# Fifteen small loads at the head of ScalarE's DMA queue in a streaming row-normalisation kernel

## The chip, the cores and the metric

The kernel runs on one core of one Trainium2 chip. The metric is device time in microseconds (us). The times shown are whole-launch times; the span of a profile runs from the first to the last instruction of one profiled execution.

## The reference

The input `x` has the shape (32, 512, 1024) in float32, that is 16384 rows of 1024 elements, 67.11 MB. Each row is divided by the sum of its absolute values, and the result has the same shape.

```
sums = np.sum(np.abs(x), axis=-1, keepdims=True)
return (x / (sums + 1e-8)).astype(np.float32)
```

## The kernel before

All of `x` is read once and all of the output is written once. The 16384 rows are 128 for each of 128 partitions. They are cut into eleven pieces: ten with 12 rows per partition (6144 KB) and a last one with 8 rows per partition (4096 KB). Pieces 0, 1 and 10 lie in the first 32 x 128 rows of the input, where partition p owns 32 rows one after the other; each of the others is a block of 12 x 128 rows. In this text piece i's load is called L0 to L10 and its store S0 to S10.

One loop runs over the pieces. A piece gets one of four buffers (`BUFS = 4`, tile `x_tile`, 48 KB per partition). SyncE issues the load (line 88). VectorE (DVE) then takes the row sums of absolute values (line 52), adds the epsilon (line 59), takes the reciprocal (line 61) and multiplies most rows in place (lines 63 and 70); ScalarE (ACT) multiplies a few rows of the first three and the last two pieces (line 73, by the table `split`). ScalarE then issues the store (line 91). So loads stand in SyncE's DMA queue, called q1 in the profile, and stores in ScalarE's, called q10. A buffer's next load waits until the store of its last piece has landed, so L4 waits for S0, L5 for S1, and so on.

The order on each engine is the program's order. One more thing sets who waits for whom. Tile, the layer in which the kernel is written, has eight completion semaphores for the DMAs of both queues and gives them out in turn, in the order in which it plans the DMAs; a DMA that takes over a semaphore waits on its engine's queue until the DMA that last had it is complete. In the built program before, the first DMAs have these semaphores, and none of L0 to L3 waits for anything:

```
sem 0: L0   sem 1: L1   sem 2: L2   sem 3: S0
sem 4: L3   sem 5: S1   sem 6: L4   sem 7: S2   then L5 on 0, L6 on 1, ...
```

Of the kernel before, what the change touches and what calls it, by code (L numbers as in the profile page):

```python
# [1 line left out]

# [4 lines left out]

FP32 = mybir.dt.float32
EPS = 1e-8


@with_exitstack
def kernel(
    ctx: ExitStack,
    tc: tile.TileContext,
    x: bass.AP,
    out: bass.AP,
):
    nc = tc.nc
    P = nc.NUM_PARTITIONS  # L20

    x_flat = x.flatten_outer_dims()
    out_flat = out.flatten_outer_dims()
    n, d = x_flat.shape

    R = 12
    BUFS = 4  # L30
    HEAD = 32
    per_partition = n // P
    assert n % P == 0 and (per_partition - HEAD) % R == 0
    rows = [R] * ((per_partition - HEAD) // R + 2) + [HEAD - 2 * R]

    def piece(flat, i):
        head = flat[: P * HEAD, :].rearrange("(p r) d -> p r d", p=P)
        if i < 2:
            return head[:, R * i : R * (i + 1), :]
        if i == len(rows) - 1:  # L40
            return head[:, 2 * R :, :]
        a = P * (HEAD + R * (i - 2))
        return flat[a : a + P * R, :].rearrange("(p r) d -> p r d", p=P)

    sbuf = ctx.enter_context(tc.tile_pool(name="sbuf", bufs=BUFS))
    stats = ctx.enter_context(tc.tile_pool(name="stats", bufs=len(rows)))

    def normalize(x_tile, k, kv, kt):


        s = stats.tile([P, R], FP32)
        nc.vector.tensor_reduce(  # L52
            out=s[:, :k],
            in_=x_tile[:, :k, :],
            axis=mybir.AxisListType.X,
            op=mybir.AluOpType.add,
            apply_absolute_value=True,
        )
        nc.vector.tensor_scalar_add(out=s[:, :k], in0=s[:, :k], scalar1=EPS)  # L59
        inv = stats.tile([P, R], FP32)  # L60
        nc.vector.reciprocal(out=inv[:, :k], in_=s[:, :k])  # L61
        if kv:
            nc.vector.tensor_mul(  # L63
                out=x_tile[:, :kv, :],
                in0=x_tile[:, :kv, :],
                in1=inv[:, :kv].unsqueeze(2).to_broadcast([P, kv, d]),
            )
        for r in range(kv, kv + kt):
            row = x_tile[:, r, :]
            nc.vector.tensor_scalar_mul(out=row, in0=row, scalar1=inv[:, r : r + 1])  # L70
        for r in range(kv + kt, k):
            row = x_tile[:, r, :]
            nc.scalar.activation(  # L73
                out=row,
                in_=row,
                func=mybir.ActivationFunctionType.Copy,
                scale=inv[:, r : r + 1],
            )

    last = len(rows) - 1
    split = {0: (3, 4), 1: (0, 3), 2: (0, 3), last - 1: (0, 2), last: (5, 3)}

    with tc.manual_schedule():
        for i, k in enumerate(rows):
            x_tile = sbuf.tile([P, R, d], FP32)
            nc.sync.dma_start(out=x_tile[:, :k, :], in_=piece(x_flat, i))  # L88
            kt, ks = split.get(i, (0, 0))
            normalize(x_tile, k, k - kt - ks, kt)  # L90
            nc.scalar.dma_start(out=piece(out_flat, i), in_=x_tile[:, :k, :])


# [1 line left out]
_INS = ['x']  # L95
_OUTS = [((32, 512, 1024), 'float32')]


# [23 lines left out]
```

## Time and profile before

| what | value |
|---|---|
| time of the runs | 316.94 and 317.59 us, median 317.26 us |
| span of the profiled execution | 315.8 us |
| VectorE busy | 261.2 us, 83% of the span |
| ScalarE busy | 17.4 us |
| bytes moved | 134.22 MB, 425 GB/s over the span |
| q1 (loads), q10 (stores), share of 16 DMA engines | 49.8% and 49.1% |

The profile's page states no launch time of its own for the profiled execution: what stands beside its span is the median of the runs, 1.46 us above it. The trace holds, beside instructions, a record of every DMA packet: queue, start, duration, bytes. A load or a store of 12 rows is 128 packets of 49152 bytes, one per partition, and sixteen packets of 4 bytes, which raise its completion semaphore.

### The profile page before, as it was taken

The numbers are of one execution on the slowest core, as the hardware profiler recorded it, in microseconds if no ns is written. First come the engines' busy times: TensorE is split into PE (matmuls) and PEld (weight loads), VectorE is DVE, ScalarE is ACT, GpSimd is POOL, SyncE is SP. The second block draws the span as 40 slices with busy tenths as digits, with TensorE's granted clock in tenths as the row PEclk, the third lists the DMA queues.
The fourth block names the chain that finished last, engine by engine and source line by source line (L and its number), as shares of the span: only waits on it lengthen the run. The fifth ranks groups of instructions, "written<-read, shape, count | busy, mean of one in ns | idle before, by whom it ended". The sixth has DMA issues, their size and how long they took to land.

```text
span 315.8 us, 168 instructions
## 1 busy us (share of the span) xinstructions
DVE 261.2 (83%) x51; ACT 17.4 (6%) x16; POOL 0.2 (0%) x4
## 2 busy tenths in 40 slices
DVE  0079999999999999969996999799699969999200
ACT  0010404004000000000000000000000000201200
POOL 0000000000000000000000000000000000000000
DMA  8999999999999999999999999999999999999986
GB/s 324 473 398 448 448 361 430 405 486 405 405 486 405 405 486 411 423 467 405 448 436 411 479 405 411 473 417 405 473 417 411 467 413 450 421 442 423 473 374 282
DMA packets 3168, 134.22 MB, mean 425 GB/s; under 512 B 352, under 2 KB 352, under 8 KB 352
## 3 DMA queue, kind: packets, MB, share of 16 engines
q1 hardware_dynamic: 1584, 67.11, 49.8%
q10 hardware_dynamic: 1584, 67.11, 49.1%
HBM read 67.11 MB, written 67.11 MB: 425 GB/s over the span
## 4 chain that ended last, share of the span: by engine, by line
DVE 41%; DMA 33%; another core or an unknown queue 18%; issue 0%; SPq 0%; DVEq 0%
DVE s L52 23%; DMA x_tile<-in_x_dram 17%; DMA out_dram<-x_tile 16%; DVE x_tile L63 15%; DVE x_tile L70 1%; DVE inv L61 0%; DVE s L59 0%; SPq L88 0%; DVEq L117 0%
## 5 line engine op out<-in xcount | busy, mean ns | idle before, releaser
L52 DVE TENSOR_REDUCE s<-x_tile 128x12 f32<-128x12288 f32 (+1 forms) x11 | 138.2, 12561 | 31.5 <-DMA x_tile<-in_x_dram 31.5
L63 DVE TENSOR_TENSOR x_tile<-x_tile,inv 128x12288 f32<-128x12288 f32 (+3 forms) x10 | 113.6, 11358 | 0.5
L73 ACT ACTIVATE x_tile<-x_tile,inv 128x1024 f32<-128x1024 f32 x15 | 16.1, 1138 | 258.7 <-DVE inv L61 258.7
L70 DVE TENSOR_SCALAR x_tile<-x_tile,inv 128x1024 f32<-128x1024 f32 x8 | 5.5, 748 | 0.0
L61 DVE RECIPROCAL inv<-s 128x12 f32<-128x12 f32 (+1 forms) x11 | 2.5, 226 | 0.4
L73 ACT ACT_TABLE_LOAD x1 | 1.3, 1283 | 17.7 <-DMA x_tile<-in_x_dram 17.7
L59 DVE TENSOR_SCALAR s<-s 128x12 f32<-128x12 f32 (+1 forms) x11 | 1.9, 173 | 0.4
L106 POOL MEMSET const-bfloat16-1.0<- 128x1 bf16 x1 | 0.1, 102 | 0.0
L106 POOL MEMSET const-uint8-127<- 128x1 uint8 x1 | 0.1, 102 | 0.0
L106 POOL MEMSET const-float32-0.0<- 128x1 f32 x1 | 0.1, 99 | 0.2 <-issue 0.2
L106 POOL MEMSET const-float32-1.0<- 128x1 f32 x1 | 0.1, 99 | 0.0
## 6 DMA issues: line engine op xcount, KB each, us to landing
x_tile<-in_x_dram SPq DMA_DIRECT2D x10, 6144.0 KB, 38.0
out_dram<-x_tile ACTq DMA_DIRECT2D x10, 6144.0 KB, 47.4
x_tile<-in_x_dram SPq DMA_DIRECT2D x1, 4096.0 KB, 33.3
out_dram<-x_tile ACTq DMA_DIRECT2D x1, 4096.0 KB, 20.6
```

The costliest lines, as they stand in the source:

```text
L52: nc.vector.tensor_reduce(out=s[:, :k], in_=x_tile[:, :k, :], axis=mybir.AxisListType.X, op=mybir.AluOpType.add, apply_absolute_value=True,)
L59: nc.vector.tensor_scalar_add(out=s[:, :k], in0=s[:, :k], scalar1=EPS)
L61: nc.vector.reciprocal(out=inv[:, :k], in_=s[:, :k])
L63: nc.vector.tensor_mul(out=x_tile[:, :kv, :], in0=x_tile[:, :kv, :], in1=inv[:, :kv].unsqueeze(2).to_broadcast([P, kv, d]),)
L70: nc.vector.tensor_scalar_mul(out=row, in0=row, scalar1=inv[:, r : r + 1])
L73: nc.scalar.activation(out=row, in_=row, func=mybir.ActivationFunctionType.Copy, scale=inv[:, r : r + 1],)
L106: nc = _bacc.Bacc("TRN2", target_bir_lowering=False, num_devices=1)
```

## The change

Before anything else, ScalarE issues fifteen small loads into a new scratch tile `tag`. Number n (called Tn here) copies the first 128 elements of the first n rows of `x`, 512 bytes each, to the first n partitions of `tag`; together they are 120 rows and 61,440 bytes. Nothing reads `tag`.

The loop is also written differently: four loads are written ahead of it, and in it L(i+4) follows S(i). The instructions on SyncE and on VectorE, and their order, are the same as before; ScalarE has the fifteen DMA issues more, ahead of its activation-table load.

```
     with tc.manual_schedule():
-        for i, k in enumerate(rows):
-            x_tile = sbuf.tile([P, R, d], FP32)
-            nc.sync.dma_start(out=x_tile[:, :k, :], in_=piece(x_flat, i))
-            kt, ks = split.get(i, (0, 0))
-            normalize(x_tile, k, k - kt - ks, kt)
-            nc.scalar.dma_start(out=piece(out_flat, i), in_=x_tile[:, :k, :])
+        tag = ctx.enter_context(tc.tile_pool(name="tag", bufs=1)).tile([P, 15, 128], FP32, name="tag")
+        for n in range(1, 16):
+            nc.scalar.dma_start(out=tag[:n, n - 1, :], in_=x_flat[:n, :128])
+        for i in range(BUFS):
+            load(i)
+        for i in range(len(rows)):
+            compute(i)
+            store(i)
+            if i + BUFS < len(rows):
+                load(i + BUFS)
```

`load`, `compute` and `store` hold the same calls as the old loop's body. In the built program after, the fifteen loads take their turns at the eight semaphores too, and waits on SyncE's and ScalarE's queues follow from it:

```
sem 0: T1, T8, L1      sem 1: L0, T9, L2      sem 2: T2, T10, S0     sem 3: T3, T11, L3
sem 4: T4, T12, S1     sem 5: T5, T13, L4     sem 6: T6, T14, S2     sem 7: T7, T15, L5
ScalarE's queue: T1 ... T7 wait for nothing; T8 waits for T1, T9 for L0, T10 for T2, ... T15 for T7
SyncE's queue:   L0 waits for nothing; L1 waits for T8, L2 for T9, L3 for T11
```

From there on each DMA takes over a semaphore from a load or a store well ahead of it, as before.

More of the change, by code (lines that the diff above doesn't have):

```diff
@@ L83, with load, store, compute @@
     split = {0: (3, 4), 1: (0, 3), 2: (0, 3), last - 1: (0, 2), last: (5, 3)}
-    with tc.manual_schedule():
-        for i, k in enumerate(rows):
-            x_tile = sbuf.tile([P, R, d], FP32)
-            nc.sync.dma_start(out=x_tile[:, :k, :], in_=piece(x_flat, i))
-            kt, ks = split.get(i, (0, 0))
-            normalize(x_tile, k, k - kt - ks, kt)
-            nc.scalar.dma_start(out=piece(out_flat, i), in_=x_tile[:, :k, :])
+    tiles = {}
+    def load(i):
+        x_tile = tiles[i] = sbuf.tile([P, R, d], FP32, name="x_tile")
+        nc.sync.dma_start(out=x_tile[:, : rows[i], :], in_=piece(x_flat, i))
+    def store(i):
+        nc.scalar.dma_start(out=piece(out_flat, i), in_=tiles[i][:, : rows[i], :])
+    def compute(i):
+        k = rows[i]
+        kt, ks = split.get(i, (0, 0))
+        normalize(tiles[i], k, k - kt - ks, kt)
+    with tc.manual_schedule():
+        tag = ctx.enter_context(tc.tile_pool(name="tag", bufs=1)).tile([P, 15, 128], FP32, name="tag")
[8 more added lines that the diff above has]
+                load(i + BUFS)
 _INS = ['x']
```

## Prediction

> **What bounds the kernel now.** I began with the page's sliced view, which gives the busy share of each engine in 40 equal slices, and the queue view under it.
>
> ```profile
> span 315.8 us, 168 instructions
> DVE 261.2 (83%) x51; ACT 17.4 (6%) x16; POOL 0.2 (0%) x4
> ...
> DVE  0079999999999999969996999799699969999200
> ...
> DMA  8999999999999999999999999999999999999986
> ...
> q1 hardware_dynamic: 1584, 67.11, 49.8%
> q10 hardware_dynamic: 1584, 67.11, 49.1%
> ```
>
> The reader should see that the DMA row reads 9 from the second slice to the 38th, and that the two queues add to 98.9% of sixteen engines. VectorE has holes, the DMA engines have none. Who waits for whom agrees:
>
> ```profile
> DVE s L52 <- DMA x_tile<-in_x_dram: 31.5, 7, 17.6
> ```
>
> VectorE waits 31.5 us for loads, 17.6 of them for L0; nothing waits long for VectorE. The windowed view, with the DMA share in the next-to-last column and GB/s in the last, shows the same by stage:
>
> ```profile
> 2.00:17.00 15.00, 0.00 (x0) 0.00 (x0) 0.00 (x0) 1.00 0.90 390
> 17.00:20.00 3.00, 2.35 (x1) 1.28 (x1) 0.00 (x0) 1.00 1.02 442
> 20.00:38.00 18.00, 17.90 (x7) 4.27 (x4) 0.00 (x0) 1.00 1.01 437
> ...
> 60.00:120.00 60.00, 59.22 (x10) 3.23 (x3) 0.00 (x0) 1.00 1.01 436
> 120.00:180.00 60.00, 54.22 (x9) 0.00 (x0) 0.00 (x0) 1.00 1.00 433
> ```
>
> (A packet is counted where it starts, hence values beside 1.) The packet records give the bound exactly. A packet of 49152 bytes takes 1.815 us whether it loads or stores, one of 32768 bytes 1.213, one of 4 bytes 0.009. Each engine has 160 of the first, 16 of the second: 160 x 1.815 + 16 x 1.213 = 309.8 us. The first packet starts 1.73 us into the span, the last ends at 314.39, and 1.41 us follow. What is left, 315.8 - 309.8 - 1.7 - 1.4 = 2.9 us, is slow packets: the first of each engine (2.04 to 2.67 us, mean 2.49, so 0.67 over the usual) and the one in which the store queue starts, at 40.5 us (2.94 to 3.61, some 1.2 over), on all sixteen engines, and a few scattered ones of about 2.1 us. So nothing but idle or slower DMA engines can lengthen this kernel, and a stall of all sixteen at any point is added to its end.
>
> **The change part by part.** The sum is made against the profiled execution's span, 315.8 us; the median of the runs, 317.26, is 1.46 higher, and I add the difference to that.
>
> *The loop's new form* moves no instruction on SyncE or VectorE: 0 us.
>
> *The fifteen issues on ScalarE.* A store's issue there takes 0.34 to 0.38 us:
>
> ```profile
> L91 ACTq DMA_DIRECT2D out_dram<-x_tile x11: 338/338/378, 38.7 to 294.1; - x11
> ```
>
> Fifteen are 15 x 0.36 = 5.4 us. ScalarE's first work is a table load at 17.7 us and its first activation at 31.1, when VectorE has the reciprocals:
>
> ```profile
> 17.70 1.28 ACT L73 ACT_TABLE_LOAD   x1 [17.70 <-DMA x_tile<-in_x_dram]
> ...
> 31.10 4.27 ACT L73 ACTIVATE x_tile<-x_tile,inv 128x1024 f32<-128x1024 f32 x4 [12.12 <-DVE inv L61]
> ```
>
> T1 to T7 go out from 0.7 to 3.2 us. T8 follows when T1 has landed. T9 waits for L0 and holds T10 to T15, the table load and the activations behind it: out at 17.6, done issuing at 17.6 + 7 x 0.36 = 20.1, table loaded at 21.4, still 9.7 us ahead of the activation. Cost 0; without VectorE's 13.4 us of sums as cover, 3.7 us.
>
> *Bytes.* No packet of 512 bytes is in the trace. From below it is the 4-byte packet, 0.009 us. From above, it might stall an engine as a queue's first packet does, 0.67 us over. A line through 4 bytes and 49152 bytes gives 0.028 us; I take that, since packets of both sizes follow each other without a gap. With its semaphore packet a tag is 0.037 us per engine. If the engine with most of them gets one row of each, that is 15 x 0.037 = 0.6 us (bounds 0.3 and 10.2). Engines ended between 313.0 and 314.4, so part of this falls into another engine's lead: 0.3 us.
>
> *The wait of L1 for T8*, the dear part. Before, SyncE had all four first loads out at once:
>
> ```profile
> 0.73 1.89 SPq L88 DMA_DIRECT2D x_tile<-in_x_dram  x4
> 17.65 12.95 DVE L52 TENSOR_REDUCE s<-x_tile 128x12 f32<-128x12288 f32 x1 [17.65 <-DMA x_tile<-in_x_dram]
> ```
>
> L1's first packets began the moment L0's last ended, at 16.85 to 17.28 us, mean 17.05. Now L1 is issued only when T8 has landed, and L2 and L3 are queued behind it on SyncE. How long does T8 take? Where both queues hold work, an engine's packet records alternate strictly: one load packet, one store packet, and a 4-byte packet takes a turn of its own. So while L0 is under way, an engine does one packet of a tag for every 1.815 us packet of L0. L0 has eight packets and a semaphore packet on each engine. T1 to T8 have, on an engine that gets a row of each, 8 x 2 = 16 packets. When L0 is done there at about 17, only some 8 of the 16 are. The other 8, tiny, follow at once, 0.2 us, and the semaphore shows 0.35 us later (L0's last 4-byte packets ended up to 17.27, it landed at 17.62). T8 lands at about 17.6, when L0 does.
>
> SyncE then issues L1. From issue to first packet the start of the kernel took 1.0 to 1.64 us, mean 1.14: first packets at 17.62 + 1.14 = 18.76, 1.71 later than before. The rings have run dry, so I charge the first packet's 0.67 again: 1.71 + 0.67 = 2.4 us, bounds 1.7 (soonest start, 0.2 over) and 3.3 (latest, 0.86 over), and nothing if T8 lands before 16.
>
> What is late next? L2 waits for T9, which goes out with L0's landing at 17.6 and meets empty rings: L2 is out by 20 to 24 us, while L1 runs to about 34. L3 needs T11, six more turns of 1.815 at worst, about 30 us, while L2 runs to 48. S0 needs T10, which is there before 38.7. VectorE needs L1 at 38.6 and gets it at 34. So one gap, not three, and VectorE sees nothing; it has 8 us of lead at the end too (the last store is issued at 294.1, its packets begin at 303).
>
> *The store queue's slow start.* The 1.2 us at 40.5 may be the price of q10's first use, then paid under T1 to T7 (-1.2), or that of the first write, then unchanged. I take 0, keeping -1.2 as the lower end.
>
> The sum: 315.8 + 2.4 + 0.3 = 318.5 us of span; as a run 317.26 + 2.7 = 320.0 us.
>
> **A rule weighed.** The alternation above is the row. The Trainium skill, "DMA: Bandwidth & Descriptors", section "Queues, rings and completion order", says that an engine takes a whole packet of typically 9 to 17 descriptors from one ring before it turns to the next. If a turn took so many tag descriptors, T1 to T8 would pass in two turns, T8 would land near 9 us, L1 would be queued in time, and by the rule the sum would be about 317.6; by the row it is 320.0. I follow the row, in which even two records of one queue, data and semaphore, are two turns.
>
> **The rivals.**
>
> *No gap (chance 0.26).* T8 lands before L0's last packet. For it: T1 to T7 might pass ahead of L0, both queues starting at the same barrier, or several small packets might go in one turn; L0's issue of 0.53 us is the longest on SyncE. Against it: the alternation, and T8 can go only after T1 has landed, with twelve packets of T2 to T7 ahead of it. Time: 317.26 + 0.3 = 317.6, or 316.4 if the store queue's 1.2 us go too.
>
> *Small packets stall (chance 0.13), the slower side.* Each tag's read is exposed on the engine that has all fifteen, as a queue's first packet is, 0.67 us each: 15 x 0.67 = 10 us on that engine, which every load and store must wait for, and 2.4 for the gap: 317.26 + 12.4 = 329.7 us. It decides the 2% from (6.3 - 2.4) / 15 = 0.26 us per tag. For it: both queue starts in the trace were slow on all sixteen engines. Against it: 4-byte packets between large ones cost 0.009 us, 352 times, and no switch between the queues after 40.5 us cost anything.
>
> *Faster (0.02).* With 309.8 us of packets, 1.7 before and 1.4 after, a span under 309.5 isn't possible unless packets get faster than 1.815 us, which none was in the record of before.
>
> **How the numbers follow.** The forecast, one gap, has 0.59. The time is 320.0. Its own bounds are 1.7 + 0 and 3.3 + 0.6, or 319.0 to 321.2. The range takes in no gap with the store start saved, 316.4, at the lower end; at the upper it goes part of the way to the stall, to 323.5, or 0.25 us per tag, leaving the dear half of that rival outside. Two per cent, about what a measurement of this kernel tells from no change, is 310.9 to 323.6. Faster 0.02; slower the stall's 0.13 and a remainder of 0.02 for a gap that repeats; within 2%: 0.83.
>
> **What would show it.** Right: SyncE's second load issued near 17.6 us instead of in the first 2.6, the windowed DMA share well under 0.9 between 17 and 20 us and 1.0 from there, packets of 1.815 us afterwards, VectorE's second reduce still at about 38.6, the last store about 2.7 us later. No gap: the second issue before 16 us. Stall: one engine's queue far behind the other fifteen, loads landing late on one increment of sixteen, and DMA shares under 1 after 20 us. The forecast is wrong altogether if L1 goes out in the first 3 us, or if VectorE's waits after 60 us grow by more than a few us.

## The result and the profile after

The changed kernel takes 320.84 us (two runs, 320.63 and 321.05) against 317.26: the ratio is 1.0114, 95% interval 1.0098 to 1.013. The profiled execution took 320.63 us at a span of 318.9 us, 3.1 us over the span before. The forecast was 320.0.

The sliced view of the changed kernel, busy tenths in 40 equal slices, with its queue lines:

```profile
span 318.9 us, 182 instructions
...
DVE  0079999999679969996998899699969979999700
...
DMA  8959999999999999999999999999999999999997
...
q1 hardware_dynamic: 1584, 67.11, 49.6%
q10 hardware_dynamic: 1824, 67.17, 48.7%
```

One digit of the DMA row is new: the third slice, 16 to 24 us, reads 5 where it read 9. From there on the row is what it was, but for the last two slices, where the engines now end closer together. The windowed view puts a finer ruler on it; the next-to-last column is the DMA share:

```profile
2.00:17.00 15.00, 0.00 (x0) 0.00 (x0) 0.00 (x0) 1.00 0.86 371
17.00:20.00 3.00, 2.05 (x1) 0.00 (x0) 0.00 (x0) 1.00 0.64 204
20.00:38.00 18.00, 17.90 (x6) 5.55 (x5) 0.00 (x0) 1.00 0.96 406
...
60.00:120.00 60.00, 53.00 (x10) 3.23 (x3) 0.00 (x0) 1.00 1.00 434
120.00:180.00 60.00, 54.63 (x9) 0.00 (x0) 0.00 (x0) 1.00 1.01 436
```

Between 17 and 20 us the DMA engines moved 204 GB/s instead of 442. Who made them wait stands in the waits of SyncE's queue (total, times, longest), and the order of the first 40 us in the timeline:

```profile
SPq L82 <- DMA tag<-in_x_dram: 18.3, 3, 17.6
```

```profile
0.72 19.92 ACTq L96 DMA_DIRECT2D tag<-in_x_dram  x15
0.73 19.66 SPq L82 DMA_DIRECT2D x_tile<-in_x_dram  x4
17.95 12.95 DVE L47 TENSOR_REDUCE s<-x_tile 128x12 f32<-128x12288 f32 x1 [17.95 <-DMA x_tile<-in_x_dram]
20.67 1.28 ACT L68 ACT_TABLE_LOAD   x1 [20.67 <-DMA tag<-in_x_dram]
...
38.81 12.95 DVE L47 TENSOR_REDUCE s<-x_tile 128x12 f32<-128x12288 f32 x1
38.97 0.38 ACTq L85 DMA_DIRECT2D out_dram<-x_tile  x1
```

The four first loads, out within 1.89 us before, now stretch over 19.66 us. The instruction records behind that row give L0 at 0.73, L1 at 18.67, L2 at 19.29, L3 at 20.06. L1 went out 0.01 us after T8's last increment, at 18.66. In the timeline before, VectorE's second reduce stands at

```profile
38.50 12.94 DVE L52 TENSOR_REDUCE s<-x_tile 128x12 f32<-128x12288 f32 x1
```

and now at 38.81, later by the 0.3 us by which the first reduce was late too (17.95 against 17.65): the gap never reached it.

The time can be added up from the packet records. L1's first packets start at 19.90 us on the mean of the engines, 2.85 later than before (17.05), and take 2.32 us instead of 1.815, 0.50 more. That is 3.36 us. The mean end of the sixteen engines moved by 3.77, from 313.41 to 317.18. The last engine, which sets the span, moved only by 3.03, from 314.39 to 317.42, since before four engines ended 0.7 to 1.4 us after the rest and here none did.

### The profile page after: what moved, and what is told of

Same layout as the page of the kernel before. It is cut to its first block, busy times and chain, and to the rows that moved or that the text cites. A ratio compares the mean times of both kernels' runs of the same rounds, so it can differ in the third digit from the quotient of the medians.

```text
span 318.9 us, 182 instructions
## 1 busy us (share of the span) xinstructions
DVE 261.4 (82%) x51; ACT 17.4 (5%) x16; POOL 0.2 (0%) x4
## 4 chain that ended last, share of the span: by engine, by line
DMA 71%; DVE 21%; issue 1%; ACT 1%; DVEq 0%; SPq 0%
DMA x_tile<-in_x_dram 60%; DVE s L47 19%; DMA out_dram<-x_tile 11%; DVE x_tile L65 1%; DVE x_tile L58 1%; ACT x_tile L68 1%; DVEq L129 0%; DVE inv L56 0%; DVE s L54 0%; SPq L82 0%
```

## The experiments

Theory A: the loss is a gap of all sixteen engines between L0 and L1. T8 has given its semaphore to L1; T8's packets get one turn for each packet of L0; so it lands only after L0 has ended. Rivals: B, the small packets or their bytes slow the engines; C, the new form of the loop; D, a like amount for each small load. Each kernel was timed against the kernel before on the same chip, 317.4, 317.7 and 317.8 us in the three groups of runs.

**The loop alone.**

```
-        for n in range(1, 16):
-            nc.scalar.dma_start(out=tag[:n, n - 1, :], in_=x_flat[:n, :128])
```

> The changed kernel without the fifteen small loads: only the loop's new form is left. Theory A (the time went into a gap between L0 and L1, because L1 takes over T8's completion semaphore): 317.3 us, within 0.5 of before. Rival B (the small packets themselves slow the engines): the same 317.3. Rival C (the new form of the loop costs it): 320 to 321.

Measured: 317.16 us, ratio 0.9992 (0.9981 to 1.0003). C is out: the loss is in the fifteen loads.

**The same loads on another queue.**

```
-            nc.scalar.dma_start(out=tag[:n, n - 1, :], in_=x_flat[:n, :128])
+            nc.gpsimd.dma_start(out=tag[:n, n - 1, :], in_=x_flat[:n, :128])
```

> The same fifteen small loads, issued on GpSimd's queue, whose DMAs have completion semaphores of their own; SyncE's L0 to L3 wait for nothing. Same rows, same bytes. Theory A: 317.3 to 317.9 us, SyncE's four loads issued in the first 3 us, no gap near 17 us. Rival B: packets cost what they cost, 320 to 321 us.

Measured: 317.82 us, ratio 1.0002 (0.9984 to 1.0019). The timeline shows SyncE's four loads together again:

```profile
0.74 1.93 SPq L82 DMA_DIRECT2D x_tile<-in_x_dram  x4
```

**The same rows in three DMAs**, still first on ScalarE's queue.

```
-        for n in range(1, 16):
-            nc.scalar.dma_start(out=tag[:n, n - 1, :], in_=x_flat[:n, :128])
+        for n in range(3):
+            nc.scalar.dma_start(out=tag[:8, 5 * n : 5 * n + 5, :],
+                in_=x_flat[:40, :128].rearrange("(p r) d -> p r d", p=8))
```

> The same 120 rows of 512 bytes, still on ScalarE's queue and at the same place, but in three DMAs of 8 partitions x 5 rows. With three instead of fifteen, no semaphore is handed on within the first four loads, so L1 waits for nothing. Theory A: 317.3 to 318.0 us. Rival B: 320 to 321 us, since packets and bytes are those of the changed kernel, and on eight engines with 15 rows each rather than on one.

Measured: 317.1 us, ratio 0.9993 (0.9983 to 1.0002). In the windows the engines never pause:

```profile
17.00:20.00 3.00, 1.98 (x1) 1.28 (x1) 0.00 (x0) 1.00 1.21 511
20.00:38.00 18.00, 17.90 (x6) 4.27 (x4) 0.00 (x0) 1.00 1.01 433
```

120 packets of 512 bytes among L0 to L2 cost nothing that can be seen. B is out.

**The gap alone**, with no small load on ScalarE.

```
         load(0)
+        nc.sync.dma_start(out=tag[:1, 0, :], in_=tiles[0][:1, 0, :128])
         for i in range(1, BUFS):
             load(i)
```

> No small loads on ScalarE. On SyncE one 512-byte copy out of piece 0's buffer stands between L0 and L1; it waits for L0's landing at 17.6 us, so L1 is issued at about 18.0. Theory A: first packets of L1 at about 19.2 us in place of 17.05, and 0.5 for the slow first packet: +2.2 + 0.5 = 2.7, or 320.0 us, with VectorE's waits for loads about twice that longer. Rival B: no small packets to speak of, so 317.3 to 317.6 us; it also holds that VectorE or the stores absorb a gap this early.

Measured: 320.95 us, ratio 1.0133 (1.0097 to 1.0169); the profiled execution took 320.26. That is 0.9 above theory A's figure: the gap came out longer than I gave it, and the six runs scatter from 320.26 to 323.82, which is taken up below. The timeline shows the wait made by hand, the windows the hole:

```profile
0.73 0.38 SPq L82 DMA_DIRECT2D x_tile<-in_x_dram  x1
17.72 0.58 SPq L96 DMA_DIRECT2D tag<-x_tile  x1
17.72 12.95 DVE L47 TENSOR_REDUCE s<-x_tile 128x12 f32<-128x12288 f32 x1 [17.72 <-DMA x_tile<-in_x_dram]
18.35 1.50 SPq L82 DMA_DIRECT2D x_tile<-in_x_dram  x3
```

```profile
17.00:20.00 3.00, 2.28 (x1) 1.28 (x1) 0.00 (x0) 1.00 0.76 246
```

L1's first packets start at 19.70, 2.65 late, and run 0.57 long: 3.22 us. The engines' mean end moved by 3.21. One 512-byte copy on the load queue costs about what fifteen small loads cost, when it holds the same load back.

**How many loads it takes.** With n small loads, L1 takes over the semaphore of T(n-7). Only the count changes:

```
-        for n in range(1, 16):
+        for n in range(1, 11):     # and 12, 13, 14, 15: T1 to T11, T12, T13, T14
```

> Only T1 to T10. The semaphores then fall so that L1 takes over T3's, L2 T4's and L3 T6's. In the changed kernel's trace T3 has landed at 12.2 us, while L0 is under way until 17. Theory A (a gap through T8's semaphore): L1 is queued before L0 ends, no gap, 317.3 to 317.9 us. Rival D (each small load costs a like amount, on whichever engine or queue): 10/15 of 3.6, that is 319.7 us.

> T1 to T11: L1 takes over T4's semaphore. T4 landed at 15.94 us in the changed kernel and with ten loads alike, and a load's first packets come 1.0 to 1.6 us after its issue, while L0 ends at 16.9 to 17.3. Theory A: L1 is out at 16.0, just in time, 317.4 to 318.0 us: the step between no loss and nearly all of it lies between eleven loads and twelve. Rival D (a like amount for each load): 11/12 of what twelve cost, 321.9 us.

> T1 to T12. L1 takes over T5's semaphore. In the changed kernel's trace T5 landed at 18.1 us, T8 at 18.66. Theory A: L1 out 0.55 us sooner than in the changed kernel and fewer small packets, so 319.9 to 320.6 us: most of the loss is back with two loads more than ten. Rival D: 12/15 of 3.6, that is 320.1 us, but then ten must give 319.7.

> T1 to T13: L1 takes over T6's semaphore and goes out about 0.2 us later than with twelve. Theory A alone, by the mean end of the sixteen engines: 320.0 to 320.5 us. Theory E (a gap of about 2 us, as with twelve loads and with single rows, leaves one engine some 2.7 us behind the other fifteen by the end, a gap of 2.6 us does not): 322 to 323 us, one engine ending over 2 us after the median.

> T1 to T14: L1 takes over T7's semaphore, about 0.2 us later still, a gap of some 2.4 us. Theory A alone: 320.2 to 320.8 us. Theory E: between thirteen (with a straggling engine) and fifteen (without one), so 320.5 or 322 to 323, and the engines' last packets tell which.

| small loads | L1 waits for | L1 issued, us | L1's first packets late + long, us | mean end of the engines, against before | time, us | ratio (95%) |
|---|---|---|---|---|---|---|
| 10 | T3 | 12.25 | 0.07 + 0.01 | +0.1 | 317.49 | 0.9998 (0.9989 to 1.0007) |
| 11 | T4 | 15.81 | 0.68 + 0.48 | +1.5 | 320.34 | 1.0091 (1.0065 to 1.0117) |
| 12 | T5 | 17.78 | 1.99 + 0.50 | +2.9 | 322.3 | 1.0154 (1.014 to 1.0168) |
| 13 | T6 | 18.06 | 2.12 + 0.67 | +3.0 | 321.26 | 1.0124 (1.0106 to 1.0142) |
| 14 | T7 | 18.29 | 2.36 + 0.64 | +3.2 | 321.7 | 1.0133 (1.0117 to 1.0149) |
| 15 | T8 | 18.67 | 2.85 + 0.50 | +3.8 | 320.84 | 1.0114 (1.0098 to 1.013) |

The last row is the changed kernel, two runs, against the 317.26 us it was first compared with.

Ten loads cost nothing, though they too hold all four first loads apart: by the timeline only three of them are out in the first 20 us,

```profile
0.72 17.78 ACTq L96 DMA_DIRECT2D tag<-in_x_dram  x10
0.73 15.56 SPq L82 DMA_DIRECT2D x_tile<-in_x_dram  x3
```

but each goes out while its predecessor still has packets to move. Twelve cost most of it by the mean end (2.9 of 3.8 us) and more than all of it by the time. D is out. My figure for eleven was a miss: L1 issued 1.0 us before the first engine was done with L0 was not in time, its first packets came 1.9 us after the issue on the mean, and they were slow even on engines that had not stood idle. With ten, L1 went out 4.6 us before the first engine was done, and that was ample; the limit lies between.

The times of twelve, thirteen and fourteen don't rise with the gap and lie 0.8 to 1.7 us above what theory A gave, and that expectation fell as well. The mean end of the engines does rise; what is added is one engine that ends late, 2.6, 1.7 and 1.5 us after the mean, where with fifteen it is 0.2. Its records show a load packet of 1.9 to 2.6 us now and then, from 72 to 275 us.

**Fifteen single rows.**

```
-            nc.scalar.dma_start(out=tag[:n, n - 1, :], in_=x_flat[:n, :128])
+            nc.scalar.dma_start(out=tag[:1, n - 1, :], in_=x_flat[:1, :128])
```

> Fifteen small loads as before, each of one row only: 15 rows of 512 bytes in place of 120. L1 still takes over the eighth's semaphore. Theory A: what counts is that an engine which takes a row of every one gives each two turns between packets of L0; the eighth lands at about 18.7 us again, 320.3 to 320.9 us. Rival B (bytes or packets): an eighth of them, 317.7 us.

Measured: 321.99 us, ratio 1.0141 (1.0121 to 1.0161). The eighth landed at 18.16, sooner than I gave it, L1 went out at 18.18, and its packets came 2.34 late and 0.55 long. One engine that is given a row of each DMA is enough; an eighth of the rows makes the same hole. The mean end moved by 3.1 us; the rest is a straggler again, 2.8 us after the mean.

**A longer gap, twice.** Two copies in place of one, and a copy that waits for VectorE's sums, neither with small loads on ScalarE. Of the second edit only the lines that make the gap are shown: a list `sums` keeps each piece's `s`, and the loop leaves `compute(0)` out.

```
+        nc.sync.dma_start(out=tag[:1, 1, :], in_=tiles[0][:1, 1, :128])   # a second copy
```

```
         load(0)
+        compute(0)
+        nc.sync.dma_start(out=tag[:1, 0, :8], in_=sums[0][:1, :8])        # sums[0]: piece 0's s
```

> As the run with one copy between L0 and L1 on SyncE, with two such copies: L1 goes out 0.5 to 0.6 us later, a gap of 3.2 us and 0.5 for the slow first packet. Theory A: 0.6 more than with one copy, 321.4 to 321.8 us against 320.95. If the stragglers hang on the small loads and not on the gap, no engine ends over 1 us after the median here; if they come at random, they may come here too.

> No small loads on ScalarE. On SyncE a 32-byte copy of piece 0's row sums stands between L0 and L1, so L1 is issued when VectorE has them, at about 31.2 us; its first packets come at about 32.5, 15.5 us later than before, and 0.5 for the slow first packet: a gap of 16 us. Theory A in its plain form (a gap of all engines is added to the end): 333.3 us. Theory A2 (loads that are late meet the stores, get every second packet and lose twice the gap, as VectorE's timeline in the changed kernel shows; once that uses up the last store's lead of 9.2 us, the end pays double for the rest): 2 x 16 - 9.2 = 22.8, or 340 us.

Two copies: 321.48 us, ratio 1.0133 (1.0113 to 1.0154). L1's packets 3.14 late and 0.68 long, sum 3.82; mean end +3.9, as A has it. But one engine ended 1.9 us after the mean, with no small load in the program and a gap of 3.1 us; so E, which tied the stragglers to a gap of about 2 us, fell.

The long gap: 335.05 us, ratio 1.0556 (1.0503 to 1.061); the profiled execution 333.3. Its windows show sixteen engines at rest:

```profile
17.00:20.00 3.00, 2.24 (x1) 1.28 (x1) 0.00 (x0) 1.00 0.00 0
20.00:38.00 18.00, 17.90 (x7) 4.26 (x4) 0.00 (x0) 1.00 0.34 131
```

15.84 late and 0.64 long make 16.5; the mean end moved by 16.5. The plain form of A holds over a factor of fourteen in the gap, and A2, double pay once the last store's lead is gone, was wrong: the last store was still queued over 4 us before its turn came. (The factor counts from the 1.2 us of eleven loads.) The four runs alone wouldn't settle it: two took 333.2 and 333.3 us, as A has it, and two, of which there is no trace, 336.8 and 337.4, between A and A2's 340.

What stays open is the straggler. Over all these profiles the last engine ends 0.2 to 2.8 us after the mean, 1.0 in the kernel before. It appeared with small loads (11 to 14, single rows) and without them (two copies), and stayed away with fifteen and with one copy. That holds for the one traced run of each kernel. The times of the others scatter: 320.26 to 323.82 us with one copy, 333.24 to 337.42 with the long gap, 319.09 to 321.88 with eleven loads, while 54 of the 55 runs of the kernel before lie between 316.7 and 318.4 (one took 320.0). So it may come and go from run to run of one kernel and need not belong to a number of loads; that the scatter is the straggler isn't shown. No run here showed what decides it. Among the traced runs it moves a time by 0.8 us down to 1.8 us up against the kernel before, as much as half the effect; so the readings above go by the mean end, which agrees with late + long to about 0.4 us in every kernel.

## Why the prediction was right

*The bound.* Right, and it carried everything: with no idle in the DMA engines before, a gap of 3.4 us came out as 3.1 in the span and 3.6 in the runs. In the gap kernels the engines' mean end moved by 3.2 for 3.2 and by 16.5 for 16.5. One reading on the way was too short: I wrote that nothing waits long for VectorE, but the waits before have

```profile
ACT x_tile L73 <- DVE inv L61: 258.7, 5, 192.4
```

ScalarE, with 17.4 us of work, waited most of the span for VectorE's reciprocals. That doesn't touch the bound, since the DMA engines had no idle time meanwhile.

*The loop, the issues on ScalarE.* Right at 0. The table load came at 20.67 us, 10.7 before the first activation at 31.41 (20.1 was forecast for the end of the issues; the last was done at 20.64).

*The turns.* Right. The packet records show 512 bytes, a packet of L0, 4 bytes, a packet of L0, and so on; the last of T4 landed at 15.93, so eight of the sixteen packets had passed when L0 was done, as counted: T1's two ahead of L0's first packet, the other six in turns with L0's. The Trainium skill, "DMA: Bandwidth & Descriptors", section "Queues, rings and completion order", has an engine drain a whole packet, typically 9 to 17 descriptors, from one ring before it switches. These records show one at a turn, and the time is that of the row; in the run with three DMAs, where an engine has five rows of one DMA, a packet of the loads stands between each two of them as well.

*When T8 lands.* The term that was mis-sized. I gave the other eight packets 0.2 us and the semaphore the usual 0.35, and had T8 land with L0 at 17.6. The packets did run through in 0.4 us, the last record ending at 17.39, but the last increments came one after the other, T5 at 18.11, T6 at 18.29, T7 at 18.47, T8 at 18.66: 0.18 us for each small load instead of the 0.037 that its two packets last. L0's last, at 17.93, stands at the same distance ahead of T5's. Why they come so far apart no run here shows. So T8 came 1.05 us late. The first packets then followed 1.23 us after the issue (1.14 forecast), at 19.90 instead of 18.76, and were 0.50 long (0.67 forecast). The term is 3.36 where I had 2.4, just above its upper bound of 3.3. (Taken against the mean of 17.05, the prediction's own rows give 3.1 for that bound, 17.62 + 1.64 - 17.05 + 0.86, and 1.8 in place of 1.7 for the lower one.)

*Bytes.* A packet of 512 bytes lasted 0.025 or 0.027 us in 114 of 120 records and 0.033 in the others, near the line's 0.028. The small loads that drained after 24 us, between packets of L1 and L2, made neighbours of mostly 1.83 to 1.92 us out of 1.815, which cost 0.27 us on the mean engine. The stall rival is out. That 0.27 is close to the 0.3 forecast is luck: the forecast counted the small packets' own time on the engine that has most of them, and had nothing for their neighbours.

*The store queue's start.* 1.15 us over the usual on the mean engine against 1.28 before. It went with the first stores, not with the queue's first use; 0 was right.

*What was wrong beside the sum.* I wrote that the last store would be issued about 2.7 us later; the timeline has

```profile
300.76 0.34 ACTq L85 DMA_DIRECT2D out_dram<-x_tile  x1
```

against 294.08, 6.7 us later. And VectorE's waits for loads after 60 us went from 13.8 to 20.0 us,

```profile
DVE s L47 <- DMA x_tile<-in_x_dram: 20.0, 7, 4.2
```

which I had named as a sign that the forecast is wrong altogether. It wasn't one. The stores stay where VectorE puts them, the late loads meet them and get every second turn, so a load loses more than the gap while the stores gain; the engines' total is the same. That this is how it comes about is argued from the alternation, not tested. VectorE was no bound, and the last store still stood in the queue over 6 us before its turn.

The gap's place as forecast, its cause as forecast, one term 1 us too small, and 0.7 us given back by chance at the end of the traced run, where no engine straggled: together they make 320.0 against 320.84. Without that chance the miss would have been about 1.6 us.

## What to carry to other kernels

When the DMA engines never rest, look for what can hold back the next transfer, not at the bytes that are added: 61 KB in fifteen DMAs cost 3.6 us, in three DMAs nothing. In these traces small DMAs ahead of large ones take turns with them one packet at a time, and they give their semaphores to the loads behind them; list which DMA takes over which semaphore in the built program, since that wait stands in no line of the source. And a load that must follow without a gap has to be queued some microseconds before the one ahead of it is done: here 1.0 us was too late and 4.6 us was ample.

## What was not expected of the hardware

- Increments of small DMAs that drain back to back came 0.18 us apart (T5 to T8), five times what the packets themselves last.
- The first packets of a load that finds nothing queued on the engines, or is issued only about 1 us ahead, take 0.5 to 0.7 us more than 1.815 on the mean of the engines, in every kernel here with a gap.
- In the traced runs the last engine of sixteen ends 0.2 to 2.8 us after the mean, through single load packets of 1.9 to 2.8 us; what decides it stays open, and runs of one kernel with a gap lie up to 4.2 us apart (333.24 to 337.42).
